# A two-layer hybrid decoder: the weight sums of the block products made in HBM by accumulating DMAs instead of on VectorE

## The chip, the cores and the metric

The kernel runs on one core of a Trainium2 chip. The metric is device time in microseconds (us) from launch to end on that core. Times of unprofiled runs stand beside one profiled execution, from which all views of the trace come.

## What is computed

The reference is a decoder trunk of two layers on 512 tokens of width 1024, in fp32. Cut to what matters here:

```python
def hybrid_layer(x, g_mix, w_in, sinks, w_a, w_b, w_out, g_mlp, w_up, w_down):
    h = rmsnorm(x, g_mix)
    z = h @ w_in                       # 1024 x 5888; q, k, v, retention q, k, v, g, gates a and b
    ...
    ya = sliding_window_sink_attention(aq, ak, av, sinks) @ w_a
    r = chunkwise_retention(rq, rk, rv)
    r = r * lax.rsqrt(jnp.mean(r * r, axis=-1, keepdims=True) + EPS)
    r = r.reshape(B, S, RET_V) * jax.nn.silu(rg)
    yb = r @ w_b                       # 1024 x 1024
    mixed = jax.nn.sigmoid(ga) * ya + jax.nn.sigmoid(gb) * yb
    x = x + mixed @ w_out              # 1024 x 1024
    h2 = rmsnorm(x, g_mlp)
    return x + jnp.square(jax.nn.relu(h2 @ w_up)) @ w_down   # 1024 x 4096 and back
```

The two layers run one after the other, and a last RMS norm follows.

## The kernel before

**Products in three parts.** TensorE (PE) multiplies values rounded to fp32r. To keep fp32's precision each operand is split into a high part `hi` (a rounded copy, made by ACT) and a low part `lo` (the rest, made by VectorE, DVE), and a product is three matmuls: hi by hi, hi by lo, lo by hi (`products`, L332 to L334).

**Weight units.** All weights come as units of 128 x 1024 fp32 (512 KB), 336 in all, in the order that `unit_order` lists: 46 of w_in with 4 of w_a among them, then w_b, w_out, w_up and w_down, for each layer. `load_until` issues a unit's load on SP's queue into one of three buffers `raw`; `split_until` has ACT write `hi` (L286) and DVE `lo` (L287), of which there are three each; `unit` hands them to the matmuls and keeps the split two units ahead and the load three more. SP's queue works in order: a load that waits for its buffer holds back what stands behind it.

**Pairs.** Two units of w_b, w_out or w_up that stand for two blocks of 128 output columns are multiplied as a 2 x 2 block product in Winograd's form, with 7 half products instead of 8: 19 pairs a layer, each in four `part`s. It needs four sums of the weight blocks. With w1 and w2 the two units and L and R their halves of 512 columns, they are s1 = w2R + w2L, s2 = s1 - w1L, s3 = w1L - w2R, s4 = w1R - s2. The same is done with the input (`sum_input`). `narrow_pair` (three matmuls per half product) and `wide_pair` (two: the moving operand holds hi and lo side by side, L1336 and L1337) run the seven products and join the results on DVE.

**Where the sums came from.** For most pairs (`load_part`, `add_part`) the blocks are loaded, and DVE makes the four sums (L252, L255, L259, L260) in the raw buffers and two `big` ones just ahead of the split. Five pairs a layer (`PARKED`) are done ahead: `raws_ahead` loads both units into two `big` buffers, `sums_ahead` has DVE make the sums (L241 to L244), stores them to HBM (L246), and the parts are later loaded from there (L219). `ahead` places this beside retention's projections.

**What sets the order.** The text of the program gives dependences. A scheduler of the framework orders the instructions of each engine by its own estimates, within what the dependences and `issue_after` allow. Attention and retention are generators, advanced between the matmuls of the projections (`advance`), so that PE always has products of weights to fill their waits.

**The other lines that matter.** `silu` (L978, L979) makes the retention gate from ACT's Sigmoid and a DVE multiply. `inverse_rms_halved` makes the factor of the MLP's norm; `first_hooks` calls it after the second unit of the first w_up group. Temporary tiles of 128 x 1024 come from the tag `big`, seven buffers. POOL has nothing to do but a few memsets (L691 clears a tile at the start of each layer) and one product at the end.

Of the kernel before, what the change touches and what calls it, by code (L numbers as in the profile page):

```python
# [18 lines left out]
P = 128  # L19
# [34 lines left out]
PARKED = (("w_b", 0), ("w_b", 2), ("w_out", 6), ("w_up", 4), ("w_up", 6))  # L54
# [73 lines left out]
def decoder(ctx, tc, xT, x_first, w_in, w_a, w_b, w_out, w_up, w_down, tables, decay, band, triangles, g_last, out):  # L128
# [17 lines left out]
    def big(name, dtype=F32):  # L146
        return tmp.tile([P, 2, T], dtype, tag="big", name=name, bufs=7)
# [28 lines left out]
    def raw_tile():  # L176
        return wpool.tile([P, UNIT], F32, tag="raw", name="raw")
# [8 lines left out]
    def load_until(n):  # L186
        while state["loaded"] < min(n, len(order)):
            i = state["loaded"]
            layer, name, j = order[i][:3]
            if name == "pair":  # L190
                load_part(i)
            else:
                raws[i] = raw_tile()
                for at in halves(i):
                    queue = nc.scalar if i == 0 and at.start == 0 else nc.sync
                    queue.dma_start(raws[i][:, at], weights[name][layer, j][:, at])
                    if i < 3:
                        load_x()
            state["loaded"] += 1

# [4 lines left out]

    park = {at: dram.tile([P, 4, T], F32, name="park_%s_%d" % at) for at in PARKED}

    def is_parked(i):
        return order[i][1] == "pair" and (order[i][4], order[i][2]) in park

    def load_part(i):
        layer, _, j, part, src = order[i]
        one, two = (weights[src][layer, j + a] for a in range(2))
        if is_parked(i):
            sums = park[src, j]
            raws[i] = raw_tile()
            sides = ((one[:, LEFT], sums[:, 0, :]), (sums[:, 1, :], one[:, RIGHT]), (sums[:, 2, :], sums[:, 3, :]), (two[:, LEFT],))
            for side, part_of in zip((LEFT, RIGHT), sides[part]):
                nc.sync.dma_start(raws[i][:, side], part_of)  # L219
            return  # L220
        if part == 0:
            raws[i] = raw_tile()
            nc.sync.dma_start(raws[i][:, LEFT], one[:, LEFT])
            raws[i + 3] = raw_tile()
            nc.sync.dma_start(raws[i + 3], two)
        elif part == 1:
            raws[i] = big("raw2").rearrange("p a t -> p (a t)")
            nc.sync.dma_start(raws[i][:, RIGHT], one[:, RIGHT])

    def raws_ahead(layer, src, j):  # L230

        two = [big("ahead").rearrange("p a t -> p (a t)") for _ in range(2)]
        for b, w in enumerate(two):
            nc.sync.dma_start(w, weights[src][layer, j + b])
        return two

    def sums_ahead(src, j, two):

        w1, w2 = two
        s1 = temp("ahead1")  # L240
        nc.vector.tensor_tensor(s1, w2[:, RIGHT], w2[:, LEFT], ALU.add)  # L241
        nc.vector.tensor_tensor(w2[:, RIGHT], w1[:, LEFT], w2[:, RIGHT], ALU.subtract)
        nc.vector.tensor_tensor(w1[:, LEFT], s1, w1[:, LEFT], ALU.subtract)
        nc.vector.tensor_tensor(w1[:, RIGHT], w1[:, RIGHT], w1[:, LEFT], ALU.subtract)  # L244
        for n, part in enumerate((s1, w1[:, LEFT], w2[:, RIGHT], w1[:, RIGHT])):
            nc.sync.dma_start(park[src, j][:, n, :], part)  # L246

    def add_part(i):
        part = order[i][3]
        if part == 0:  # L250
            w2 = raws[i + 3]
            nc.vector.tensor_tensor(raws[i][:, RIGHT], w2[:, RIGHT], w2[:, LEFT], ALU.add)  # L252
        elif part == 1:
            w1 = raws[i - 1]
            nc.vector.tensor_tensor(raws[i][:, LEFT], w1[:, RIGHT], w1[:, LEFT], ALU.subtract)  # L255
        elif part == 2:
            raws[i] = big("raw3").rearrange("p a t -> p (a t)")
            w1, w2, z2 = raws[i - 2], raws[i + 1], raws[i - 1]
            nc.vector.tensor_tensor(raws[i][:, LEFT], w1[:, LEFT], w2[:, RIGHT], ALU.subtract)  # L259
            nc.vector.tensor_tensor(raws[i][:, RIGHT], z2[:, RIGHT], z2[:, LEFT], ALU.subtract)  # L260

    def split_until(n):
        while state["split"] < min(n, len(order)):
            i = state["split"]
            load_until(i + 3)
            paired = order[i][1] == "pair"
            if paired and not is_parked(i):
                add_part(i)
# [19 lines left out]
            raws.pop(i - 3 if paired and not is_parked(i) else i, None)  # L288
# [98 lines left out]
    def group(name, layer, moving, evacuates, meanwhile=None):  # L387
# [3 lines left out]
        for u in range(4):  # L391
            hi, lo = unit(name, layer)
            for j in range(2):
                k = 2 * u + j
                for c, ps in enumerate(banks):
                    cols = slice(j * T + c * P, j * T + (c + 1) * P)
                    products(ps, [((hi[:, cols], lo[:, cols]), moving[k])], k == 0, k == KD - 1)
# [59 lines left out]
    def inverse_rms_halved(both, n, dest):  # L457

        ps = bank(ps_aux, "ssq")
        for i, part in enumerate(both):  # L460
            nc.tensor.matmul(ps, ones, part, start=i == 0, stop=i == len(both) - 1)
# [5 lines left out]
        for rows, cols in sides:  # L467
            for there, _ in sides:
                nc.scalar.activation(dest[there, cols], own[rows, :], AF.Copy)

# [19 lines left out]
    class Rms:  # L490
# [8 lines left out]
        def finish(self):  # L499
            self.value = tmp.tile([P, T], F32, tag="rstd", name="rstd", bufs=2)  # L500
            (inverse_rms if self.folded else inverse_rms_halved)(self.parts, D, self.value)
# [79 lines left out]
    def layer_body(layer):  # L581
# [12 lines left out]
        def sum_input(by_form, b, ks):  # L594
# [1044 lines left out]
```

## Time and profile before

| what | us |
|---|---|
| three runs, median (lowest to highest) | 1472.45 (1472.3 to 1472.51) |
| the profiled execution, its own time | 1473.8 |
| its span, first to last instruction | 1472.0 |
| PE busy | 1464.8 |
| DVE busy | 1166.7 |
| ACT busy | 810.9 |
| DMA, mean share of 16 engines on SP's queue | 40.7% |

The span is what the trace shows; the own time of that execution has 1.8 us more around it. A busy time is the union of an engine's instructions. Matmuls are pipelined and their ends modelled, so two that follow each other overlap in the records. A row such as "L287 DVE TENSOR_TENSOR lo<-raw,hi ... x291 | busy, mean ns | idle before <-releaser" gives a group of instructions: line, engine, operation, what it writes and reads, its count, its busy time, the mean of one in ns, and how long the engine had been idle before them and what ended that.

### The profile page before, as it was taken

The numbers are of one execution on the slowest core, as the hardware profiler recorded it, in microseconds if no ns is written. First come the engines' busy times: TensorE is split into PE (matmuls) and PEld (weight loads), VectorE is DVE, ScalarE is ACT, GpSimd is POOL, SyncE is SP. The second block draws the span as 40 slices with busy tenths as digits, with TensorE's granted clock in tenths as the row PEclk, the third lists the DMA queues.
The fourth block names the chain that finished last, engine by engine and source line by source line (L and its number), as shares of the span: only waits on it lengthen the run. The fifth ranks groups of instructions, "written<-read, shape, count | busy, mean of one in ns | idle before, by whom it ended". The sixth has DMA issues, their size and how long they took to land.

```text
span 1472.0 us, 20220 instructions
## 1 busy us (share of the span) xinstructions
PE 1464.8 (100%) x7466; PEld 1249.6 (85%) x7466; DVE 1166.7 (79%) x1920; ACT 810.9 (55%) x1306; POOL 3.8 (0%) x14
## 2 busy tenths in 40 slices
PE   9999999999999999999999999999999999999998
PEld 7888888888988888888888888888989888888887
DVE  7998878778988787776678986786899877878763
ACT  7656356654684445444455753656547754444553
POOL 0000000000000000000000000000000000000000
PEclk9999999999999999999999999999999999999999
DMA  6422843356443332333543258333654522333241
GB/s 227 127 89 92 300 158 99 102 172 212 126 126 118 101 115 93 104 104 115 165 126 97 86 186 272 104 104 102 207 171 126 154 95 93 114 106 109 90 140 57
DMA packets 71043, 194.45 MB, mean 132 GB/s; under 512 B 8457, under 2 KB 8609, under 8 KB 70945
## 3 DMA queue, kind: packets, MB, share of 16 engines
q1 hardware_dynamic: 70656, 192.65, 40.7%
q8 instruction: 58, 0.95, 0.3%
q10 hardware_dynamic: 288, 0.52, 0.1%
q14 instruction: 41, 0.33, 0.1%
HBM read 171.63 MB, written 18.89 MB: 129 GB/s over the span
## 4 chain that ended last, share of the span: by engine, by line
PE 94%; issue 5%; DMA 1%; DVE 0%; ACT 0%; POOLq 0%; DVEq 0%; SPq 0%
PE mm L334 22%; PE mm L332 22%; PE mm L333 22%; PE mm L1336 11%; PE mm L1337 5%; PE rv L332 2%; PE rv L333 2%; PE rv L334 2%; PE score L842 1%; PE r L332 1%; PE r L334 1%; PE r L333 1%; PE pT L797 0%; PE pv L823 0%; PE pv L824 0%
## 5 line engine op out<-in xcount | busy, mean ns | idle before, releaser
L333 PE MATMUL mm<-r,hi 128*128 128x512 f32 (+1 forms) x1568 | 572.5, 367 | 0.0
L332 PE MATMUL mm<-r,hi 128*128 128x512 f32 (+1 forms) x1568 | 569.7, 367 | 0.6 <-ACT r L342 0.6
L334 PE MATMUL mm<-r,lo 128*128 128x512 f32 (+1 forms) x1568 | 563.9, 367 | 0.2
L286 ACT ACTIVATE hi<-raw 128x1024 fp32r<-128x1024 f32 (+1 forms) x334 | 334.1, 1002 | 386.4 <-PE mm L333 206.8
L287 DVE TENSOR_TENSOR lo<-raw,hi 128x512 fp32r<-128x512 f32 (+1 forms) x335 | 384.7, 1151 | 111.6 <-ACT hi L286 107.9
L334 PEld LDWEIGHTS mm<-r,lo 128*128 128x128 f32 x1568 | 293.7, 188 | 48.7 <-DVE lo L287 1.4
L332 PEld LDWEIGHTS mm<-r,hi 128*128 128x128 f32 x1568 | 293.8, 188 | 47.5 <-ACT r L342 1.4
L333 PEld LDWEIGHTS mm<-r,hi 128*128 128x128 f32 x1568 | 294.3, 188 | 45.9
L1336 PE MATMUL mm<-r,hi 128*128 128x512 f32 x728 | 252.1, 391 | 0.0
L1337 PE MATMUL mm<-r,lo 128*128 128x256 f32 x728 | 200.5, 277 | 0.0
L1336 PEld LDWEIGHTS mm<-r,hi 128*128 128x128 f32 x728 | 136.5, 188 | 28.6
L1337 PEld LDWEIGHTS mm<-r,lo 128*128 128x128 f32 x728 | 136.7, 188 | 3.1 <-DVE lo L287 0.7
L1416 DVE TENSOR_TENSOR x<-x,mm 128x512 f32<-128x512 f32 x56 | 37.8, 686 | 28.9 <-PE mm L334 28.9
L1409 ACT ACTIVATE z<-z 128x512 f32<-128x512 f32 x56 | 32.4, 623 | 48.7 <-DVE z L1389 48.7
L333 PE MATMUL rv<-lo,r 128*128 128x512 f32 x128 | 49.8, 389 | 0.0
L334 PE MATMUL rv<-hi,r 128*128 128x512 f32 x128 | 49.5, 389 | 0.0
L332 PE MATMUL rv<-hi,r 128*128 128x512 f32 x128 | 49.4, 390 | 0.0
L340 DVE TENSOR_TENSOR r<-z,r 128x512 fp32r<-128x512 f32 x64 | 42.9, 686 | 3.0 <-ACT r L339 2.6
L339 ACT ACTIVATE r<-z 128x512 fp32r<-128x512 f32 x64 | 38.4, 619 | 7.9 <-DVE z L1070 7.8
L869 ACT ACTIVATE sm<-sm,st 128x256 f32<-128x256 f32 (+1 forms) x64 | 30.1, 472 | 18.9 <-DVE st L857 18.7
L1389 DVE SCALAR_TENSOR_TENSOR z<-z,rstd 128x512 f32<-128x512 f32 x52 | 35.7, 687 | 0.6
L340 DVE TENSOR_TENSOR r<-sums,r 128x1024 fp32r<-128x1024 f32 x24 | 28.9, 1220 | 0.0
(273 smaller groups left out, 1693.0 us busy)
## 6 DMA issues: line engine op xcount, KB each, us to landing
raw<-w_in_in SPq DMA_DIRECT2D x89, 512.0 KB, 3.7
raw<-w_down_in SPq DMA_DIRECT2D x64, 512.0 KB, 3.6
raw<-w_up_in SPq DMA_DIRECT2D x32, 512.0 KB, 4.0
raw<-w_up_in SPq DMA_DIRECT2D x60, 256.0 KB, 2.9
raw<-w_a_in SPq DMA_DIRECT2D x8, 512.0 KB, 4.8
ahead<-w_b_in SPq DMA_DIRECT2D x8, 512.0 KB, 5.4
park_w_b<-ahead SPq DMA_DIRECT2D x16, 256.0 KB, 5.7
ahead<-w_up_in SPq DMA_DIRECT2D x8, 512.0 KB, 4.9
```

Of the source, the lines that this page charges most:

```text
L286: nc.scalar.activation(hi[:, at], raw[:, at], AF.Copy)
L287: last_low[:] = [nc.vector.tensor_tensor(lo[:, at], raw[:, at], f32(hi[:, at]), ALU.subtract).ins]
L332: nc.tensor.matmul(ps, ah, bh, start=start and i == 0, stop=False, **more)
L333: nc.tensor.matmul(ps, ah, bl, start=False, stop=False, **more)
L334: nc.tensor.matmul(ps, al, bh, start=False, stop=stop and i == n - 1, **more)
L339: nc.scalar.activation(hi, src, AF.Copy)
L340: nc.vector.tensor_tensor(lo, src, f32(hi), ALU.subtract)
L1336: nc.tensor.matmul(both, hi[:, c], m, start=start and k == 0, stop=False, **more)
L1337: nc.tensor.matmul(ps[:, :H], lo[:, c], m[:, 0, :], start=False, stop=k == 3 and start, **more)
L1389: nc.vector.scalar_tensor_tensor(z[:, :, at], z[:, :, at], 0.0, factor, ALU.max, ALU.mult)
L1409: nc.scalar.activation(z[:, i, :], z[:, i, :], AF.Square)
L1416: nc.vector.tensor_tensor(x[:, c, :], x[:, c, :], ps, ALU.add)
```

## The change

All 19 pairs of both layers get their sums from HBM, and no engine adds them. `sum_weights` issues, per pair, four DMAs from HBM to HBM on SP's queue, which copy w2R three times and w1R once into a fresh tensor of four parts, and then five accumulating DMAs on POOL's queue (`accum_op=ALU.add`), each adding 256 KB to a part. [...] The input's second row of sums, the joins, the relu (`ALU.min` for a negated value) and the updates of x take a sign.

When the sums are issued follows from estimated start times of the units (2.45 us for a part of a pair, 5.45 for any other): the n-th pair's at 45 + 33 n us, or 60 us before the estimated load of the pair, whichever is earlier. They stand behind the last load issued by then.

Beside that: four raw buffers instead of three, with loads four ahead of the split; six `big` buffers instead of seven; Silu as one ACT instruction; the end of the MLP's norm (`rms_mlp.finish`) moves into the fourth unit of the first w_up group, with its second half of matmuls held behind the norm's sum.

```diff
-PARKED = (("w_b", 0), ("w_b", 2), ("w_out", 6), ("w_up", 4), ("w_up", 6))
+SUMS_FROM, SUMS_EVERY, SUMS_BEFORE = 45.0, 33.0, 60.0
...
-        return tmp.tile([P, 2, T], dtype, tag="big", name=name, bufs=7)
+        return tmp.tile([P, 2, T], dtype, tag="big", name=name, bufs=6)
...
-        return wpool.tile([P, UNIT], F32, tag="raw", name="raw")
+        return wpool.tile([P, UNIT], F32, tag="raw", name="raw", bufs=4)
...
             state["loaded"] += 1
+            if sums_due and sums_due[0][0] <= starts[i]:
+                with tc.issue_after(last_load[0]):
+                    sum_weights(sums_due.pop(0)[1])
...
+    starts = [0.0]
+    for u in order:
+        starts.append(starts[-1] + (2.45 if u[1] == "pair" else 5.45))
+    pairs_at = [i for i, u in enumerate(order) if u[1] == "pair" and u[3] == 0]
+    sums_due = [(min(starts[i] - SUMS_BEFORE, SUMS_FROM + n * SUMS_EVERY), i) for n, i in enumerate(pairs_at)]
+    sums, last_load = {}, []
+
+    def sum_weights(i):
+
+        layer, _, j, _, src = order[i]
+        one, two = (weights[src][layer, j + a] for a in range(2))
+        dest = dram.tile([P, 4, T], F32, name=f"sums_{src}_{layer}_{j}")
+        s = [dest[:, n, :] for n in range(4)]
+        every = [P, 2, T]
+        for part in s[:3]:
+            nc.sync.dma_start(part, two[:, RIGHT])
+        nc.sync.dma_start(s[3], one[:, RIGHT])
+        for first, block in ((0, two), (1, one)):
+            for n in range(first, first + 2):
+                nc.gpsimd.dma_start(s[n], block[:, LEFT], accum_op=ALU.add)
+        nc.gpsimd.dma_start(s[3], s[1], accum_op=ALU.add)
+        sums[i] = dest
...
+        made = sums.pop(i - 3) if part == 3 else sums[i - part]
+        raws[i] = raw_tile()
+        sides = ((one[:, LEFT], made[:, 0, :]), (made[:, 1, :], one[:, RIGHT]), (made[:, 2, :], made[:, 3, :]), (two[:, LEFT],))
+        for side, part_of in zip((LEFT, RIGHT), sides[part]):
+            last_load[:] = [nc.sync.dma_start(raws[i][:, side], part_of).ins]
...
-            load_until(i + 3)
+            load_until(i + 4)
             paired = order[i][1] == "pair"
-            if paired and not is_parked(i):
-                add_part(i)
...
+                with tc.issue_after(between()) if between and (u, j) == (3, 1) else nullcontext():
+                    for c, ps in enumerate(banks):
...
-            split(*parts_of_forms(0), f[0].rearrange("p (j k) t -> p j k t", k=2))
+            split(*parts_of_forms(0), f[0].rearrange("p (j k) t -> p j k t", k=2), -1.0)
...
-            nc.vector.tensor_tensor(t4, b21, t2, ALU.subtract)
+            nc.vector.tensor_tensor(t4, t2, b21, ALU.subtract)
...
-            ins = nc.vector.tensor_tensor(z[:, 1, SECOND], b, eu[:, :H], ALU.add).ins
+            ins = nc.vector.scalar_tensor_tensor(z[:, 1, SECOND], b, -1.0, eu[:, :H], ALU.mult, ALU.subtract).ins
...
-            s = temp("sig")
-            nc.scalar.activation(s, rg[i], AF.Sigmoid)
-            nc.vector.tensor_tensor(rg[i], rg[i], s, ALU.mult)
+            nc.scalar.activation(rg[i], rg[i], AF.Silu)
...
-                rms_mlp.finish()
-                sum_input(by_form, scaled_pair(2, g_mlp), 2)
...
-                late = group("w_up", layer, xs, [put_up] * 4, first_hooks())
+                late = group("w_up", layer, xs, [put_up] * 4, first_hooks(), rms_mlp.finish)
```

The code of `raws_ahead`, `sums_ahead`, `add_part`, `is_parked` and `ahead` is gone.

More of the change, by code (lines that the diff above doesn't have):

```diff
@@ L1 @@
 from contextlib import ExitStack
+from contextlib import nullcontext
 from functools import partial
@@ L195, in load_until @@
                     queue = nc.scalar if i == 0 and at.start == 0 else nc.sync
-                    queue.dma_start(raws[i][:, at], weights[name][layer, j][:, at])
+                    load = queue.dma_start(raws[i][:, at], weights[name][layer, j][:, at]).ins
+                    if queue is nc.sync:
+                        last_load[:] = [load]
                     if i < 3:
@@ L213, in load_part @@
         one, two = (weights[src][layer, j + a] for a in range(2))
[L214 to L246, printed above, removed]
@@ L385, in chunk, with group @@
         evacuate(ps)
[L387 removed]
+    def group(name, layer, moving, evacuates, meanwhile=None, between=None):
         banks = [bank(ps_mm, "mm") for _ in range(4)]
@@ L460, in inverse_rms_halved @@
         for i, part in enumerate(both):
-            nc.tensor.matmul(ps, ones, part, start=i == 0, stop=i == len(both) - 1)
+            summed = nc.tensor.matmul(ps, ones, part, start=i == 0, stop=i == len(both) - 1).ins
         own = temp("own")[:, : T // 2]
@@ L1126, in layer_body @@
                 silu(i)
-        def ahead():
-            if to_sum:
-                with tc.issue_after(last_low[0]):
-                    sums_ahead(*to_sum.pop(0))
-            load_ahead()
-        qk(1, between=ahead)
-        values(0, ahead)
+        qk(1)
+        values(0)
         aT = [(a_h[:, c, :], a_l[:, c, :]) for c in range(4)]
@@ L1273, in add_to_x, with put @@
         def add_to_x(c):
-            def put(i, at, src, z):
+            def put(i, at, src, z, sign=1.0):
                 own = x[:, c + i, at] if isinstance(i, int) else x[:, c : c + 2, at]
-                return nc.vector.tensor_tensor(own, own, src, ALU.add)
+                return nc.vector.tensor_tensor(own, own, src, ALU.add if sign > 0 else ALU.subtract)
             return put
```

74 lines of the change are left out of this document (28 added, 46 removed).

## The prediction

> **What bounds the kernel now.** I read the page's busy shares and its chain of work first, then the stretches view for the places where TensorE (PE) is not busy, then PE's own waits, then the chain around a gap.
>
> ```profile
> span 1472.0 us, 20220 instructions
> PE 1464.8 (100%) x7466; PEld 1249.6 (85%) x7466; DVE 1166.7 (79%) x1920; ACT 810.9 (55%) x1306; POOL 3.8 (0%) x14
> PE 94%; issue 5%; DMA 1%; DVE 0%; ACT 0%; POOLq 0%; DVEq 0%; SPq 0%
> ```
>
> PE is busy for 1464.8 of 1472.0 us, and the chain that ended last is 94% PE and 5% issue between matmuls. DVE, ACT and DMA hold at most 1% of it. The stretches say where the missing 7.2 us lie; the columns are the stretch, its length, then busy us of PE, PEld, DVE, ACT, POOL, the granted clock, DMA share and GB/s.
>
> ```profile
> 0.00:50.00 50.00, 48.33 (x203) 39.33 (x204) 40.02 (x56) 35.03 (x56) 1.92 (x12) 1.00 0.62 202
> 50.00:350.00 300.00, 300.00 (x1483) 254.46 (x1482) 245.69 (x465) 169.96 (x296) 0.00 (x0) 1.00 0.45 148
> 350.00:400.00 50.00, 49.91 (x331) 45.69 (x330) 46.84 (x69) 29.08 (x43) 0.00 (x0) 1.00 0.48 153
> 400.00:1100.00 700.00, 700.00 (x3473) 593.66 (x3472) 555.40 (x911) 377.92 (x599) 0.96 (x1) 1.00 0.41 132
> 1100.00:1150.00 50.00, 49.91 (x336) 45.88 (x335) 46.41 (x66) 37.73 (x55) 0.00 (x0) 1.00 0.39 117
> 1150.00:1400.00 250.00, 250.00 (x1303) 213.98 (x1302) 196.62 (x299) 128.93 (x196) 0.00 (x0) 1.00 0.35 109
> 1400.00:1472.00 72.00, 66.67 (x348) 56.60 (x346) 35.73 (x61) 32.28 (x61) 0.90 (x1) 0.99 0.29 95
> ```
>
> From 50 to 1400 us PE lacks 0.09 + 0.09 = 0.18 us. The start lacks 1.67 us and the end 5.33 us. A busy PE can hide a short stall, because a matmul's modelled end reaches past the next one's start, so I looked for such stalls in the chain (start us, us, what):
>
> ```profile
> 389.34 0.13 PE mm L334
> ...
> 389.84 0.74 DVE r L343
> ...
> 391.10 1.23 DVE lo L287
> 392.33 0.04 issue
> 392.38 0.38 PE mm L334
> 392.76 0.12 PE mm L332
> ```
>
> One matmul there stands for 0.38 us where its neighbours take 0.12 to 0.13: 0.26 us lost behind DVE, where the MLP of layer 0 begins. I count four such places at most (two at each of the two MLP starts), 1.0 us. So the most that an edit away from start and end can bring is about 0.18 + 1.0 = 1.2 us. The matmuls themselves are the same 7466 in the changed program.
>
> **The change part by part.** *Arithmetic taken off DVE.* Four adds make a pair's sums; 28 pairs make them in place and 10 ahead of time (first and last of each four shown), and 16 gates lose a multiply.
>
> ```profile
> L252 DVE TENSOR_TENSOR raw<-raw 128x512 f32<-128x512 f32 x28 | 19.3, 691 | 7.4 <-DMA raw<-w_up_in 6.5
> L260 DVE TENSOR_TENSOR raw<-raw 128x512 f32<-128x512 f32 x28 | 19.3, 689 | 0.6
> L241 DVE TENSOR_TENSOR ahead<-ahead 128x512 f32<-128x512 f32 x10 | 6.9, 687 | 1.8 <-DMA ahead<-w_up_in 1.6 <-DMA ahead<-w_b_in 0.2
> L244 DVE TENSOR_TENSOR ahead<-ahead 128x512 f32<-128x512 f32 x10 | 6.9, 688 | 0.1
> L979 DVE TENSOR_TENSOR z<-z,sig 128x512 f32<-128x512 f32 x16 | 10.7, 686 | 3.5 <-ACT sig L978 3.5
> L1389 DVE SCALAR_TENSOR_TENSOR z<-z,rstd 128x512 f32<-128x512 f32 x52 | 35.7, 687 | 0.6
> L978 ACT ACT_TABLE_LOAD x2 | 2.6, 1283 | 0.2 <-DVE z L970 0.2
> ```
>
> 4 x 19.3 + 4 x 6.9 + 10.7 = 115 us less of DVE's 1167. Of that PE gets only what it waits for, at most the 1.2 us above; I credit half, 0.6 us, because the stall shown hangs on two DVE steps in a row and only the load beside them gets lighter. The sign edits turn an add into a form with a factor, 687 ns in L1389 for what a plain add of that size takes (686): nothing. *Gates.* Sigmoid becomes Silu, one ACT instruction each as before; by the built program's order ACT loads its function table 23 times instead of 19, 4 x 1.283 = 5.1 us on an engine with 661 us idle. Without that cover it would be 5.1 us.
>
> By the Trainium skill, "ScalarE: Activation LUTs", What ACT_TABLE_LOAD costs, a switch is the 1283 ns load and a drain of about 1380 ns, so 10.7 us by the page. The row agrees on 1283 and shows 0.2 us idle before, so the trace decides for 5.1.
>
> *Buffers.* The fourth weight buffer takes what the seventh "big" buffer gives. Two of the seven served the sums and the loads ahead, which are gone, so six are no tighter: nothing. Should a filler be held up, PE's order has room: the attention's last product comes 31 matmuls after the start of the next stage, before 16; 15 products of at most 0.38 us, 6 us, if nothing ran beside them.
>
> *Moved step.* The end of the MLP's norm goes from the second weight unit to inside the fourth: its sums, square root and copies land beside PE in either place. Nothing; the bound is that 1.0 us of hidden stalls, either way.
>
> *DMA.* This is the large part. Per pair the new code issues four copies HBM to HBM, five accumulating DMAs, and loads seven halves of 256 KB instead of what was 1 MB.
>
> ```profile
> q1 hardware_dynamic: 70656, 192.65, 40.7%
> raw<-w_up_in SPq DMA_DIRECT2D x32, 512.0 KB, 4.0
> raw<-w_up_in SPq DMA_DIRECT2D x60, 256.0 KB, 2.9
> park_w_up<-ahead SPq DMA_DIRECT2D x16, 256.0 KB, 7.3
> ```
>
> 192.65 MB cost 40.7% of 1472 us on all engines, 3.11 us per MB; 256 KB is 0.262 MB. A pair not parked before costs 0.79 MB more to load, 2.4 us; its copies 1.05 MB, 3.3 us; five accumulations of 0.262 MB, 4.1 us if priced as plain transfers. No trace shows an accumulating DMA. It reads two operands and writes one, so its work lies between one plain transfer and three in a row: 4.1 to 12.2 us a pair; a gain is excluded. I take two (8.2), halfway. Its landing lies between a load (2.9) and two loads and a store (2.9 + 2.9 + 7.3 = 13.1); I take 7.3, the row that also writes HBM beside other traffic.
>
> By the Trainium skill, "Collectives: The Full Stack", The bandwidth ceiling, an adding DMA is not slowed by its add but by needing two reads on one ring, which halves its rate. By that page alone a pair's accumulations cost 8.2 us. No run here shows it yet.
>
> What lies beside it, per stretch; the last two lines are pieces of the chain that recur once a pair and two down units:
>
> ```profile
> 300.00:350.00 50.00, 50.00 (x303) 44.70 (x302) 39.40 (x50) 26.19 (x36) 0.00 (x0) 1.00 0.61 197
> 450.00:650.00 200.00, 200.00 (x1018) 170.30 (x1017) 155.39 (x238) 98.83 (x147) 0.00 (x0) 1.00 0.31 101
> 1050.00:1100.00 50.00, 50.00 (x296) 44.43 (x296) 41.89 (x57) 22.70 (x30) 0.00 (x0) 1.00 0.66 218
> ```
>
> ```profile
> 485.57 0.46 PE mm L334 x2
> ...
> 506.06 0.46 PE mm L334 x2
> ```
>
> In the MLP a cycle lasts 506.06 - 485.57 = 20.5 us, 31% of it DMA: 6.4 us, plus 2.4 for the loads. By the rule in the code sums come every 33 us, and for the last six pairs of layer 0 every 20.7. There the sums add 3.3 + 8.2 = 11.5: 20.3 of 20.5 us, full (16.2 at one transfer, 24.3 at three). Elsewhere 11.5 x 20.5/33 = 7.1: 15.9 of 20.5. In the stretches with w_b and w_out, 30.5 to 33 us of 50 are busy; two pairs' loads add 4.8 and 1.5 sums 17: 53 to 55 of 50, late by 3 to 5 us (nothing at one transfer, 9 to 11 at three).
>
> What PE has in hand: four raw buffers and three split ones put a load seven units ahead of PE, six after its buffer comes free. In the MLP six units are 20.5 us, less 4.0 landing and two splits by ACT and DVE:
>
> ```profile
> L287 DVE TENSOR_TENSOR lo<-raw,hi 128x1024 fp32r<-128x1024 f32 x291 | 355.1, 1221 | 105.8 <-ACT hi L286 102.1 <-PE mm L334 1.9 <-DMA ahead<-w_up_in 0.2
> L286 ACT ACTIVATE hi<-raw 128x1024 fp32r<-128x1024 f32 x291 | 307.4, 1058 | 373.2 <-PE mm L333 204.6 <-PE mm L1336 100.5 <-issue 34.0
> SPq L196 <- DVE lo L287: 438.4, 119, 9.5
> ACT hi L286 <- DMA raw<-w_b_in: 6.6, 2, 3.3
> ```
>
> 2 x (1.22 + 1.06) = 4.6: about 12 us in hand. For w_out's parts (24 matmuls of 0.12 us, the fourth part half) six units are 15 us, so about 6. The SP row agrees: SP waits for DVE to free buffers (438 us), while ACT's largest wait for a weight load is 6.6 us in all. So 3 to 5 us late is covered.
>
> *The added waits.* SP waits, before a half made of sums, for POOL's accumulations, with all later weight loads behind it. The code issues sums 60 us or more ahead; copies 7.3 and three accumulations in a row 21.9 make 29: 31 spare. POOL's queue stands twice per pair for a landing and issues five DMAs:
>
> ```profile
> POOL r L691 <- PE mm L1337: 680.4, 1, 680.4
> L691 POOL MEMSET r<- x2: 947/955/963, 0.9 to 683.0; 128x1024 f32 x2
> ```
>
> With at most 0.96 us an issue (POOL's longest row), 14.6 + 4.8 = 19.4 of 20.5 us: it keeps up. The one memset in its way ran at 683 us, when layer 1's first sums begin; they are used some 290 us later. *Sum:* 1472.45 median (the profiled execution: span 1472.0, own time 1473.8, so 0.45 below and 1.35 above) less 0.6 = **1471.8**.
>
> **The rivals.** *A, DMA full (slower):* accumulations cost three transfers. w_b and w_out run 9 to 11 us late against 6 in hand: 3 to 5 lost in each layer, 6 to 10 in all, 1478 to 1482, middle **1480**; with 5 in hand it ends at 1484. In the MLP 24.3 - 20.5 = 3.8 us x 6 = 23 stay inside the 31 spare. It decides from about 2.2 transfers on. For it: the stretches are 61 to 66% busy already. Against: 3.11 us/MB contains queueing.
> *B, POOL's chain (slower):* a landing takes 13.1 us. POOL then needs 26.2 + 1.7 to 4.8 = 28 to 31 us a pair (an issue priced as SP's 0.33 or as 0.96) against 20.5; over six pairs 44 to 63 late, less 60 - 7.3 - 39.3 = 13 spare and 12 in hand: 19 to 38 lost, **1491** to 1510. It decides from about 11 us a landing. Layer 1, at 33 us, escapes. SP's issue row:
>
> ```profile
> 541.96 0.33 SPq L223 DMA_DIRECT2D raw<-w_up_in  x1
> ```
>
> *C, faster by over 0.2%:* would need 2.9 us. Only start and end hold that much, and no edit touches the first load of x or the last stores: **1469** or less.
> *D, the change doesn't spread the sums:* the built order shows 38 groups of copies between weight loads; no chance given.
>
> **How the numbers follow.** Forecast within 0.2% (2.9 us, about what a measurement of this kernel can tell from no change): 0.58. A 0.20, B 0.18, C 0.04. The range runs from full relief of the stalls and a little (1470.3) to A's end (1484) and leaves out B and most of C. Faster 0.04, same 0.58, slower 0.38.
>
> **What would show it.** Right: PE 50.00 of 50.00 from 50 to 1400 us; DVE near 1055 us; DMA share near 1.0 in 550 to 650 and near 0.8 in layer 1's MLP, with weight loads landing within 8 us; no SP wait on sums. A: PE idle in 300 to 400 and 1050 to 1150 with ACT waiting for raw. B: SP waiting on sums and PE idle in 550 to 700 only. Wrong altogether: PE idle near 0 to 300, where I expect none, or another count of matmuls.

## The result and the profile after

The changed kernel takes **1493.11 us** (median of 4 runs, 1492.68 to 1496.41) against 1472.48 (4 runs, 1472.3 to 1473.16): a ratio of **1.0142, 95% interval 1.013 to 1.0154**, 20.6 us slower. The forecast, 1471.8 with a range to 1484, was wrong. The profiled execution took 1493.07 us, with a span of 1491.0.

First the page of the changed kernel: span, busy times, queues (packets, MB, share of 16 engines), and the shares of the chain that ended last.

```profile
span 1491.0 us, 20777 instructions
...
PE 1471.3 (99%) x7466; PEld 1251.9 (84%) x7466; DVE 1061.0 (71%) x1752; ACT 817.7 (55%) x1310; POOL 160.1 (11%) x204
...
q1 hardware_dynamic: 100032, 233.56, 49.5%
q0 software_dynamic: 27360, 49.82, 23.2%
...
PE 87%; DMA 6%; DVE 3%; ACT 2%; issue 1%; SPq 0%; POOLq 0%; ACTq 0%; DVEq 0%
```

The same 7466 matmuls keep PE busy 6.5 us longer in the records and the span grew by 19.0. Of the 6.5 us some 4.5 go with a lower granted clock: its mean over the span fell from 0.999 to 0.996, and 1491 x 0.003 = 4.5, an estimate. The chain was 94% PE and 1% DMA; now it is 87% and 6%, and DVE and ACT hold 5%. The stretches of the changed kernel (columns as before: length, busy PE, PEld, DVE, ACT, POOL, clock, DMA share, GB/s) say where:

```profile
110.00:150.00 40.00, 37.39 (x174) 30.27 (x173) 30.00 (x70) 26.26 (x42) 1.63 (x2) 1.00 0.44 114
...
235.00:245.00 10.00, 9.34 (x42) 7.45 (x41) 6.75 (x10) 4.50 (x9) 0.81 (x1) 1.00 0.49 106
...
370.00:410.00 40.00, 37.20 (x271) 35.42 (x270) 31.60 (x45) 24.21 (x38) 3.29 (x4) 0.96 0.76 208
410.00:780.00 370.00, 369.95 (x1855) 313.99 (x1854) 255.12 (x370) 195.92 (x293) 48.64 (x59) 1.00 0.82 215
...
980.00:1000.00 20.00, 17.51 (x75) 14.33 (x74) 16.63 (x28) 12.16 (x20) 0.81 (x1) 0.91 0.46 118
...
1070.00:1150.00 80.00, 76.14 (x495) 68.64 (x495) 62.30 (x88) 42.49 (x62) 8.20 (x10) 1.00 0.92 255
1150.00:1400.00 250.00, 249.96 (x1294) 213.63 (x1293) 174.04 (x258) 134.31 (x201) 30.43 (x37) 1.00 0.84 211
```

In both MLPs (410 to 780, 1150 to 1400) the DMA engines are 82 and 84% busy and PE lacks 0.05 and 0.04 us. It lacks 2.61 us in attention (110 to 150), 0.66 and 2.49 in retention (235 to 245, 980 to 1000), and 2.80 and 3.86 where w_b and w_out are multiplied (370 to 410, 1070 to 1150), and at 110 to 150 and 980 to 1000 the DMA share is only 0.44 and 0.46. So "DMA full" is not the answer. PE's own waits in the changed kernel (engine, line, waited for: us in total, times, longest):

```profile
PE mm L312 <- ACT mm L622: 3.4, 2, 2.0
PE ret L312 <- DVE s L999: 2.5, 1, 2.5
PE pv L805 <- ACT r L319: 1.9, 2, 1.4
PE mm L312 <- ACT eu L625: 1.8, 2, 1.1
```

PE waits for ACT and DVE, which did not become slower (the product of z with `inv` takes 685 ns, median, before and after). What they waited for stands in the chain, here the pieces ahead of the gap at 990 us (start, us, what):

```profile
963.11 3.32 DMA row<-own
...
966.44 8.70 DMA inv<-row
...
975.17 0.76 DVE z L1046 x2
...
984.00 5.38 DMA inv<-row
...
990.69 0.48 DVE s L999
```

Retention's norm factor goes through HBM and comes back on SP's queue (`inv<-row`, 256 KB), and DVE stands still until it lands. The view of `inv` before gives 3.8 us for its landing; here one takes 8.70. (Such a view holds only landings that it can tie to their issue: for the six of the changed kernel it gives 5.4 at most, and the 8.70 of the chain is not among them. A median of landings is to be read with that in mind.) POOL's instructions at that time (start, us, line, operation, count):

```profile
965.12 2.50 POOL L231 DMA_DIRECT2D sums_w_up<-w_up_in  x3 [21.75 <-DMA sums_w_up<-w_up_in]
976.36 0.81 POOL L231 DMA_DIRECT2D sums_w_up<-w_up_in  x1 [8.74 <-DMA sums_w_up<-w_up_in]
983.57 0.81 POOL L232 DMA_DIRECT2D sums_w_up<-sums_w_up  x1 [6.39 <-DMA sums_w_up<-w_up_in]
```

Three accumulations issued within 2.5 us at 965 stand beside the load issued at 966.44, and the fifth, issued at 983.57, beside the one at 984.00. The gaps at 110 to 150 look alike: the chain ahead of them goes back to the load of a table (`rawtab`), and three accumulations were issued just ahead of it. The piece of the chain, then POOL's instructions:

```profile
105.00 10.56 DMA rawtab<-tables_in
```
```profile
103.47 2.50 POOL L231 DMA_DIRECT2D sums_w_out<-w_out_in  x3 [20.07 <-DMA sums_w_out<-w_out_in]
```

The idle time that ended with a landing of `inv<-row`, in all (us, times), is first in the kernel before, then in the changed one:

```profile
  DMA inv<-row: 8.0, 6
```
```profile
  DMA inv<-row: 19.7, 6
```

By the Trainium skill, "DMA: Bandwidth & Descriptors", Queues, rings and completion order, each DMA engine takes turns packet by packet between the queues that have work. That would make a load on SP's queue late for as long as POOL's queue has packets; the landings of 8.70 and 10.56 us agree, though no trace here shows the order of packets.

### The profile page after: what moved, and what is told of

It is laid out like the page before. It is cut to its first block, busy times and chain, and to the rows that moved or that the text cites. A ratio compares the mean times of both kernels' runs of the same rounds, so it can differ in the third digit from the quotient of the medians.

```text
span 1491.0 us, 20777 instructions
## 1 busy us (share of the span) xinstructions
PE 1471.3 (99%) x7466; PEld 1251.9 (84%) x7466; DVE 1061.0 (71%) x1752; ACT 817.7 (55%) x1310; POOL 160.1 (11%) x204
## 3 DMA queue, kind: packets, MB, share of 16 engines
q0 software_dynamic: 27360, 49.82, 23.2%
## 4 chain that ended last, share of the span: by engine, by line
PE 87%; DMA 6%; DVE 3%; ACT 2%; issue 1%; SPq 0%; POOLq 0%; ACTq 0%; DVEq 0%
PE mm L312 21%; PE mm L313 21%; PE mm L314 21%; PE mm L1299 11%; PE mm L1300 6%; DMA inv<-row 1%; DMA raw<-w_out_in 1%; PE rv L313 1%; PE rv L314 1%; PE rv L312 1%; DVE lo L267 1%; ACT hi L266 1%; DMA rawtab<-tables_in 1%; DMA gate<-aside 1%; DMA row<-own 1%
## 5 line engine op out<-in xcount | busy, mean ns | idle before, releaser
L231 POOL DMA_DIRECT2D sums_w_up<-w_up_in x112 | 92.3, 892 | 659.1 <-DMA sums_w_up<-w_up_in 651.4
L232 POOL DMA_DIRECT2D sums_w_up<-sums_w_up x28 | 22.8, 814 | 167.9 <-DMA sums_w_up<-w_up_in 167.9
```

The source lines that it names most:

```text
L231: nc.gpsimd.dma_start(s[n], block[:, LEFT], accum_op=ALU.add)
```

## The experiments

The theories after the result: **T1**, the sums' DMAs, the accumulations above all, make loads late that DVE, ACT or PE wait for at once. **T2**, the copies stand in SP's queue ahead of those loads. **T3**, one of the other edits. Times are medians; each ratio is against runs of the kernel before on the same chip, at 1472.9 to 1473.0.

| run | us | ratio, 95% interval |
|---|---|---|
| no sums | 1472.62 | 0.9998, 0.9989 to 1.0007 |
| copies only | 1473.98 | 1.0008, 0.9999 to 1.0018 |
| sums in the MLPs only | 1472.34 | 0.9996, 0.9987 to 1.0005 |
| sums outside the MLPs only | 1492.63 | 1.0131, 1.0114 to 1.0148 |
| among w_in only | 1481.68 | 1.0057, 1.0043 to 1.0071 |
| among w_b, w_out only | 1478.85 | 1.0041, 1.0027 to 1.0055 |
| small edits alone | 1475.50 | 1.0018, 1.0009 to 1.0027 |
| plain copies for accumulations | 1476.31 | 1.0024, 1.0015 to 1.0033 |
| four accumulations | 1479.08 | 1.0044, 1.0029 to 1.0059 |
| other places | 1495.22 | 1.0147, 1.0125 to 1.0169 |
| other places, four | 1490.27 | 1.0106, 1.0084 to 1.0128 |
| five, two at once | 1493.89 | 1.0144, 1.0126 to 1.0161 |
| four, three at once | 1488.90 | 1.0122, 1.0099 to 1.0146 |
| four, one at a time | 1494.97 | 1.0147, 1.0123 to 1.0172 |
| four, one at a time, evenly | 1476.61 | 1.0028, 1.0019 to 1.0037 |
| five, evenly | 1488.59 | 1.0099, 1.0084 to 1.0114 |

**No sums; copies only.**

```diff
-        made = sums.pop(i - 3) if part == 3 else sums[i - part]
-        sides = ((one[:, LEFT], made[:, 0, :]), (made[:, 1, :], one[:, RIGHT]), ...)
+        sides = ((one[:, LEFT], two[:, RIGHT]), (two[:, RIGHT], one[:, RIGHT]), ...)
```
```diff
         nc.sync.dma_start(s[3], one[:, RIGHT])
-        for first, block in ((0, two), (1, one)):
-            for n in range(first, first + 2):
-                nc.gpsimd.dma_start(s[n], block[:, LEFT], accum_op=ALU.add)
-        nc.gpsimd.dma_start(s[3], s[1], accum_op=ALU.add)
```

> The changed kernel without the nine DMAs that make a pair's sums: each part of a pair is loaded straight from the weights, so the sums in the products are left out; loads, sign rules, Silu, buffers and the moved norm stay. T1 (the sum DMAs crowd the 16 engines, so that loads which DVE, ACT or PE wait for in the attention, the retention and around w_out land late): 1471 to 1474 us, PE full from 50 to 1400. T2 (the copies stand in SP's queue ahead of those loads): the same, 1471 to 1474. T3 (the loss comes from the other edits: six big buffers, the gates' table loads, the moved norm): 1488 to 1493.

> The changed kernel with the four copies a pair on SP's queue but without the five accumulating DMAs, so the sums are left out. T1: copies are 8 of the 32 points of DMA share that the sums take, so about a quarter of the loss, 1474 to 1481 us. T2: the copies stay in SP's queue, so nearly all of the loss stays, 1487 to 1493. T3: 1488 to 1493.

Without sums the time is that of before, so T3 falls: the buffers, the table loads and the moved norm cost nothing that can be told in this kernel. It is also all that taking 104 us off DVE gives: its page has DVE at 1062.5 and PE still at 1463.9.

```profile
span 1470.5 us, 20199 instructions
...
PE 1463.9 (100%) x7466; PEld 1249.5 (85%) x7466; DVE 1062.5 (72%) x1752; ACT 817.9 (56%) x1310; POOL 3.7 (0%) x14
```

The copies alone cost about 1 us, and the interval holds none as well. That is at the lower edge of T1's 1474 to 1481, so the copies carry less of the loss than their share of the engines. T2 falls; the loss needs the accumulations.

**Where.** The sums are made only where a condition on the load then reached holds; the other pairs' parts come straight from the weights. The edit of the first of four; the others have `not` of this condition, w_in or w_a, and w_b or w_out.

```diff
+                at = sums_due.pop(0)[1]
+                if name == "w_down" or name == "w_up" or (name == "pair" and order[i][4] == "w_up"):
                     with tc.issue_after(last_load[0]):
-                        sum_weights(sums_due.pop(0)[1])
+                        sum_weights(at)
```

> The changed kernel with only those sums (17 of 38) that are issued while MLP weights are being loaded; the other 21 pairs load their parts straight from the weights, so their sums are left out. T1: in the MLP PE waits for nothing but weight loads that run seven units ahead, so 1471 to 1476 us. T2: the same cause would show in the MLP too wherever copies stand ahead of loads, 1472 to 1480. T3: 1488 to 1493.

> The complement: only the 21 sums issued while weights of w_in, w_a, w_b and w_out are being loaded; the other 17 are left out. T1: nearly the whole loss, 1487 to 1493 us, with PE idle in the attention, the retention and around w_out. T2: most of the loss, 1485 to 1493. T3: 1488 to 1493.

> Sums are made only where they fall among the loads of w_in and w_a (attention and retention); the other pairs' parts are loaded straight from the weights, so their sums are left out. Theory that each stretch loses by itself what its late loads cost: the changed kernel lost about 10 us there, so 1481 to 1485. Rival, that the loss comes only when w_b and w_out are loaded: 1472 to 1476.

> Sums are made only where they fall among the loads of w_b and w_out; the other pairs' parts are loaded straight from the weights, so their sums are left out. Theory that each stretch loses by itself: the changed kernel lost about 9 us there, so 1479 to 1484, and the excess of this run and of the one with sums among w_in add up to that of the changed kernel, 20 us. Rival, that attention and retention hold the loss: 1472 to 1476. Rival, that a backlog carried over from w_in makes the loss here: also 1472 to 1476, with the two excesses adding up to less than 15 us.

The 17 sums in the MLPs cost nothing; the other 21 cost all of it (19.6 us). Split by stage they cost 8.7 and 5.9, together 14.6: each stage loses by itself, but w_b and w_out lose a little less than expected (1479 to 1484), and 5 us of the 20 appear only with both. The place of the transfers shifts between these programs, and I did not settle which overlap makes the 5 us.

**The small edits by themselves**, in the kernel before.

```diff
-            nc.scalar.activation(s, rg[i], AF.Sigmoid)
-            nc.vector.tensor_tensor(rg[i], rg[i], s, ALU.mult)
+            nc.scalar.activation(rg[i], rg[i], AF.Silu)
...
-                late = group("w_up", layer, xs, [put_up] * 4, first_hooks())
+                late = group("w_up", layer, xs, [put_up] * 4, first_hooks(), rms_mlp.finish)
```

> The kernel before with two of the small edits alone: Silu as one ACT instruction in place of Sigmoid and a multiply, and the end of the MLP's norm moved into the fourth unit. All is computed. Theory that PE is the bound and that every hidden stall together is worth 1.2 us at most: 1471.3 to 1473.2. Rival, that the four more table loads on ACT or the matmuls held behind the norm's sum cost PE something that the run without sums made up elsewhere: 1474 to 1479.

2.6 us slower, at 1475.5: the rival's side. PE's largest wait in this run:

```profile
PE mm L333 <- ACT mm L643: 2.6, 2, 1.3
```

ACT's instructions in this run, then in the kernel before, at the end of the norm of layer 0:

```profile
425.69 1.68 ACT L471 ACTIVATE rstd<-own 64x256 f32<-64x256 f32 x4
427.39 0.37 ACT L643 ACTIVATE mm<-mm 128x256 f32<-128x256 f32 x1
```
```profile
426.21 0.37 ACT L640 ACTIVATE mm<-mm 128x256 f32<-128x256 f32 x1
426.92 1.70 ACT L469 ACTIVATE rstd<-own 64x256 f32<-64x256 f32 x4 [0.34 <-DVE own L466]
```

The scheduler now puts the norm's four copies ahead of a pair's PSUM copy that PE waits for: 1.3 us, in each layer. In the run without sums the order is the old one, and the loss is not there.

**Adding, or moving bytes?**

```diff
-                nc.gpsimd.dma_start(s[n], block[:, LEFT], accum_op=ALU.add)
+                nc.gpsimd.dma_start(s[n], block[:, LEFT])
...
-        nc.gpsimd.dma_start(s[3], s[1], accum_op=ALU.add)
+        nc.gpsimd.dma_start(s[3], s[1])
```

> The changed kernel with POOL's five DMAs as plain copies of the same 256 KB in the same order, with the same waits; the sums are left out (the parts hold copies of weights). Theory that it is the price of an accumulation (6.94 against 3.16 us of the engines per MB) that fills the engines: half of the added load stays, so 1475 to 1484. Rival, that the bytes, the second queue or POOL's waits matter and adding does not: 1488 to 1495.

1476.31, where the changed kernel has 1493: as many DMAs in the same order, with the same waits and bytes, but without the add, cost 3.4 us and not 20. POOL's queue in this run:

```profile
q0 software_dynamic: 15200, 49.82, 11.5%
```

11.5% of 1474.1 us for 49.82 MB is 3.40 us of the engines per MB; with the add it was 23.2% of 1491.0, 6.94. An accumulation costs 2.04 plain copies on the same queue. POOL's part is shorter too, 103.6 us busy against 160.1. That it takes nothing from DVE the busy times show: DVE has 1061.0 us in the changed kernel, 1061.1 here and 1062.5 without sums, where POOL has 3.7.

**Fewer accumulations; other places.** The first edit copies the second sum (w2R + w2L + w1L) from the finished first one (w2R + w2L) and then adds the last term. The second moves sums out of w_b and w_out and into layer 0's MLP.

```diff
-        for part in s[:3]:
+        for part in (s[0], s[2]):
             nc.sync.dma_start(part, two[:, RIGHT])
...
+        nc.gpsimd.dma_start(s[0], two[:, LEFT], accum_op=ALU.add)
+        nc.gpsimd.dma_start(s[2], one[:, LEFT], accum_op=ALU.add)
+        nc.gpsimd.dma_start(s[1], s[0])
+        nc.gpsimd.dma_start(s[1], one[:, LEFT], accum_op=ALU.add)
         nc.gpsimd.dma_start(s[3], s[1], accum_op=ALU.add)
```
```diff
+    early = [45.0 + 25.0 * n for n in range(8)]
+    late = [595.0 + 20.7 * n for n in range(5)] + [740.0, 800.0, 860.0]
+    due = early + [starts[i] - SUMS_BEFORE for i in pairs_at[8:19]] + late + [starts[i] - SUMS_BEFORE for i in pairs_at[27:]]
```

> The changed kernel with four accumulations and one plain copy on POOL's queue in place of five accumulations, and three copies on SP's in place of four: the second sum is copied from the finished first one, and the first weight row added to it. All is computed. Theory that the loss goes with the engines' time in accumulations: a fifth of the 20 us goes, 1486 to 1491. Rival, that what matters is that some sum is always under way beside the late loads: the same time as the changed kernel, 1491 to 1496.

> The changed kernel with the same 38 sums at other places: in layer 0 eight among the loads of w_in (seven before) and none among those of w_b and w_out; five of layer 1's moved into layer 0's MLP, three left among layer 1's w_in loads (eight before) and none among its w_b and w_out. All is computed. Theory that it is the place which decides: 11 sums among w_in at the 8.7 us that 15 cost there, or a little less where they stand further apart, and nothing else: 1477 to 1481. Rival, that the amount of DMA in the whole program decides: 1490 to 1495. Rival, that the MLP of layer 0, now with sums every 20.7 us throughout, becomes full and loses: 1484 or more with PE idle in 400 to 780.

> Both at once: the other places and four accumulations. All is computed. Theory of place and of the time in accumulations: 1476 to 1480, a little under the run with the places alone. It does not come under the kernel before (1473), as the run with sums in the MLP alone already equalled it.

All three miss the figures of the theory. With four the time is 1479: 14 of 20 us gone for a fifth of the accumulations, while POOL's queue still holds the engines for 22.7% of 1476.7, 335 us against 346. A loss in proportion to the engines' time falls. (Outside the MLPs PE lacks 0.9 us in layer 0 and 2.6 in layer 1.) The other places cost as much as the changed kernel; the stretches of that run tell why:

```profile
50.00:400.00 350.00, 349.91 (x1815) 300.26 (x1813) 272.88 (x499) 202.89 (x342) 28.64 (x35) 1.00 0.65 171
400.00:780.00 380.00, 374.46 (x1869) 316.26 (x1868) 256.85 (x372) 197.35 (x294) 68.86 (x83) 1.00 0.97 240
780.00:1150.00 370.00, 369.28 (x1902) 315.93 (x1901) 284.32 (x511) 215.72 (x357) 13.14 (x16) 1.00 0.51 144
1150.00:1400.00 250.00, 242.30 (x1237) 205.17 (x1236) 163.03 (x245) 124.25 (x187) 43.04 (x52) 0.99 0.97 233
```

Outside the MLPs PE lacks 0.09 and 0.72 us, with fewer sums there (8 and 3), though still three accumulations at once: as a cure for the late loads it worked. But with a sum every 20.7 us throughout, the MLPs' engines are 97% busy and PE lacks 5.5 and 7.7 us there. SP waits for weight loads to land (75.6 us in the largest row of its waits) and hardly for sums (2.4). That is the third expectation of that run, a second way to lose: full engines, the prediction's rival A in another place. With both edits (1490.27; runs from 1483.59 to 1491.11) PE lacks 4.75 us in layer 0's MLP at 91%, and 0.04 in layer 1's at the same 91%, so a share alone does not tell the loss here either.

**How many at once, or the fifth?** In the changed kernel POOL issues three in a row; with four accumulations, two, then one plain copy and two single ones. The three edits below: five with two at once; four with three at once; four one at a time (`add` stands for the accumulate option).

```diff
-        for first, block in ((0, two), (1, one)):
-            for n in range(first, first + 2):
-                nc.gpsimd.dma_start(s[n], block[:, LEFT], accum_op=ALU.add)
-        nc.gpsimd.dma_start(s[3], s[1], accum_op=ALU.add)
+        first = nc.gpsimd.dma_start(s[1], two[:, LEFT], accum_op=ALU.add).ins
+        with tc.issue_after(first):
+            beside = nc.gpsimd.dma_start(s[0], two[:, LEFT], accum_op=ALU.add).ins
+        with tc.issue_after(beside):
+            second = nc.gpsimd.dma_start(s[1], one[:, LEFT], accum_op=ALU.add).ins
+        with tc.issue_after(second):
+            third = nc.gpsimd.dma_start(s[2], one[:, LEFT], accum_op=ALU.add).ins
+        with tc.issue_after(third):
+            nc.gpsimd.dma_start(s[3], s[1], accum_op=ALU.add)
```
```diff
-        nc.gpsimd.dma_start(s[3], s[1], accum_op=ALU.add)
```
```diff
+        last = nc.gpsimd.dma_start(s[0], two[:, LEFT], accum_op=ALU.add).ins
+        for dest_, src_, more in ((s[1], s[0], {}), (s[1], one[:, LEFT], add), (s[3], s[1], add), (s[2], two[:, RIGHT], {}), (s[2], one[:, LEFT], add)):
+            with tc.issue_after(last):
+                last = nc.gpsimd.dma_start(dest_, src_, **more).ins
```

> The changed kernel with its five accumulations per pair, the same bytes and the same copies, but in an order on POOL's queue in which at most two are under way at once for most of the time: the first on the second sum beside the one on the first sum, then the second on the second sum beside the one on the third, then the last. In the changed kernel POOL issues three in a row. All is computed. Theory of how many are under way at once (what a late load finds ahead of it): near the run with four accumulations, 1478 to 1484. Rival, that it is the fifth accumulation itself, its time on the engines: 1490 to 1495.

> The changed kernel without the last accumulation of each pair (the fourth sum lacks its second term), the other four in the order of the changed kernel, three of them issued in a row. Theory of how many are under way at once: most of the loss stays, 1486 to 1493. Rival, that the fifth accumulation itself makes it: near the run with four accumulations, 1476 to 1482.

> Four accumulations and two plain copies on POOL's queue, each waiting for the one before but for the copy of the third sum's first term, which runs beside the fourth sum's accumulation; one copy of the first sum's term and one of the fourth's stay on SP's queue. All is computed. Theory of how many are under way at once: less than with four accumulations in pairs (1479), 1474 to 1478. Rival, that only the time on the engines counts: the same 1478 to 1481, as the bytes and the accumulations are the same.

Four with three at once lose 16 us, as the number at once says and the fifth accumulation does not. But five with two at once lose as much as the changed kernel, so two are no better than three when they follow each other in pairs. And one at a time took 1495, against 1474 to 1478 expected. Its stretches, first of early work, then of layer 0's MLP (two views):

```profile
50.00:250.00 200.00, 200.00 (x946) 167.35 (x945) 153.04 (x329) 115.04 (x215) 22.54 (x31) 1.00 0.64 151
...
800.00:1150.00 350.00, 349.90 (x1811) 300.40 (x1810) 265.72 (x474) 197.59 (x324) 37.82 (x53) 1.00 0.66 172
```
```profile
600.00:720.00 120.00, 107.08 (x512) 90.15 (x511) 64.28 (x98) 47.40 (x72) 14.90 (x20) 0.93 0.68 171
```

In 50 to 250 PE lacks nothing, and 0.10 us in 800 to 1150, which holds all of layer 1's attention, retention and w_out. The changed kernel lacked 3.27 in the first of these stretches with no more DMA:

```profile
50.00:250.00 200.00, 196.73 (x925) 163.50 (x924) 150.80 (x325) 113.64 (x212) 20.45 (x25) 1.00 0.62 153
```

What PE lacks in this run, 12.9 us, it lacks at 600 to 720. The clock there was 0.93, which is 120 x 0.07 = 8.4 us more, an estimate from that row; together they come near the 22 us that the run lost. POOL's first accumulations of three pairs in a row, and SP's wait for sums:

```profile
571.41 1.14 POOL L228 DMA_DIRECT2D sums_w_up<-w_up_in  x1
...
601.27 1.12 POOL L228 DMA_DIRECT2D sums_w_up<-w_up_in  x1
...
630.88 1.12 POOL L228 DMA_DIRECT2D sums_w_up<-w_up_in  x1
```
```profile
SPq L241 <- DMA sums_w_up<-w_up_in: 54.5, 9, 13.7
```

A pair's chain takes 29.6 to 29.9 us, and layer 0's last six pairs come every 20.5: SP waits for POOL, with all weight loads behind it. That is the prediction's rival B. So the sums were spaced evenly, first with one at a time, then in the changed kernel:

```diff
-SUMS_FROM, SUMS_EVERY, SUMS_BEFORE = 45.0, 33.0, 60.0
+SUMS_FROM, SUMS_EVERY, SUMS_BEFORE = 45.0, 29.0, 60.0
```

> The run with one accumulation at a time, with a pair's sums every 29 us of the code's estimate instead of every 33, so that layer 0's last six pairs no longer follow each other at 20.7. All is computed. Theory: that run lost nothing in attention, retention and around w_out (349.90 of 350 us of PE in 50 to 400, where the changed kernel has 353.93 of 360) and 21 us at 600 to 800 because POOL's chain takes 29.6 us a pair against the 20.5 of the MLP's pace; 29 of the estimate are 31 of the trace, so POOL keeps up: 1472 to 1477, PE full from 50 to 1400. Rival, that it lost nothing early only by chance of where the transfers fell: 1480 or more with PE idle in attention or retention again.

> The changed kernel with a pair's sums every 29 us of the code's estimate instead of every 33 and nothing else: five accumulations, three issued in a row. All is computed. Theory that it is what runs at once and not the spacing: no gain, 1488 to 1497. Rival, that the spacing makes the difference: under 1480.

1476.61 and 1488.59, each inside its range. The stretches of the run with one at a time, then those of the run with five and three at once:

```profile
50.00:400.00 350.00, 349.38 (x1807) 299.32 (x1806) 271.15 (x498) 203.45 (x342) 43.50 (x60) 1.00 0.73 182
...
780.00:1150.00 370.00, 369.90 (x1905) 316.88 (x1905) 286.73 (x506) 215.22 (x352) 47.84 (x66) 1.00 0.74 186
```
```profile
50.00:400.00 350.00, 349.72 (x1816) 300.04 (x1815) 272.70 (x499) 203.43 (x342) 41.02 (x50) 1.00 0.74 191
...
780.00:1150.00 370.00, 357.99 (x1836) 304.94 (x1835) 270.99 (x483) 202.06 (x334) 42.13 (x52) 1.00 0.72 183
```

At the same DMA shares, 0.74 and 0.72, the one lacks 0.10 us of PE at 780 to 1150 and the other 12.01. But the other lost only 0.28 in layer 0, 50 to 400. So several accumulations at once are a risk, not a fixed price: what they cost seems to depend on whether they fall on one of the few loads that are waited for, and that shifts with every edit. Taking each layer's work outside its MLP as one case (PE's missing time at 50 to 400 and at 780 to 1150): the changed kernel lost 5.4 and 6.8, five with two at once 2.1 and 10.7, four with three at once 6.1 and 3.7, four with two at once 0.9 and 2.6, five evenly 0.3 and 12.0; one at a time lost 0.1 and 2.3 (that after its backlog), and evenly 0.6 and 0.1. That waiting for each other protects those loads is likely, but not shown: these are three cases without a backlog, three at once lost as little in one case here and in the run with other places, and the chained runs also have four accumulations where the others mostly have five, and fewer copies on SP's queue. No run has five in a chain. Why five in pairs are as bad as threes is open too, and no run tells which overlap is the decisive one.

The best full form of the change, 1476.6, is still 3.6 us above the kernel before; its stretches show 1 us of it as PE's missing time. Against the run without sums its span is 4.0 us longer, and 2.1 of that lie within PE's busy time (1466.0 against 1463.9); what makes them I have not located. None beats the kernel before: the run without any sums shows nothing to be had, by its interval at most 1.6 us.

## Why the prediction was wrong

- *PE bounds the kernel, and DVE's relief is worth 1.2 us at most:* right. Without the sums 1472.62 against 1473.0, no difference that can be told; DVE at 1061 against 1055 expected (the working's own 115 us would have left 1052; 106 went).
- *Gates:* ACT went from 810.9 to 817.7 us, 6.8 against 5.1, and hidden. *Buffers:* nothing, right. *Moved norm:* nothing in this kernel, but 2.6 us in the kernel before, above the bound of 1.0 that was given "either way": a moved step changed ACT's order.
- *Price of an accumulation, two plain transfers:* right, 2.04 on one queue. By the Trainium skill, "Collectives: The Full Stack", The bandwidth ceiling, a ReduceScatter among ranks reaches about half the rate of an AllGather, because its add needs two source reads on one ring. The 2.04 agrees with that factor; it is for transfers within HBM issued by one core.
- *Landing 7.3 us, POOL keeps up, SP hardly waits for sums:* right. The landing of most of POOL's accumulations in the changed kernel (count, KB, median us), and SP's largest wait for sums (us in total, times, longest):

```profile
sums_w_up<-w_up_in POOLq DMA_DIRECT2D x112, 256.0 KB, 7.9
```
```profile
SPq L242 <- DMA sums_w_up<-w_up_in: 3.0, 5, 1.5
```

- *The MLP nearly full without loss:* right, at 0.82 and 0.84, and even at 0.97 in 550 to 600. But its 20.3 of 20.5 us "full" without loss held only for a few pairs: when the sums came every 20.7 us throughout, 97% cost PE 13 us.
- **The step that failed: "What PE has in hand".** It measured the slack of weight loads, which run seven units ahead, and set all added DMA against that. For "Elsewhere" it took 15.9 of 20.5 us busy and stopped there. It left out the loads with little or nothing in hand, which DVE or ACT waits for: `inv<-row`, `rawtab`, the gates. The trace before had `inv<-row` plainly: DVE was idle 8.0 us in all for it, six times, so a later landing went straight to DVE (19.7 us in the changed kernel) and, where the fillers ran out, to PE. The others it did not show as waits, or hardly (`rawtab` 0.2 us, the gates none); what they had in hand was never measured, and it did not cover landings of 10 us (5.5 us and 9.2 us of DVE's waits). Where the prediction had PE full it lacked 5.4 us at 50 to 400 and 6.8 at 780 to 1150. "Wrong altogether: PE idle near 0 to 300, where I expect none" is what came, at 110 to 150 and 235 to 245.
- *w_b and w_out, "late by 3 to 5 us, covered by 6":* wrong. A backlog of the engines' time was computed, but what hit was single landings. A half of w_out, issued at 394, took 10.55 us, 6.5 more than the 4.0 reckoned with, against 6 in hand (the pieces of the chain ahead of PE's wait, below); gates brought back (`gate<-aside`) at 1070 took 10.41, and PE waited 1.0 us behind them:

```profile
394.39 10.55 DMA raw<-w_out_in
...
405.04 0.63 ACT hi L266
405.67 0.28 ACT eu L625
```

- *Rivals.* A had the resource and the direction, and its sign came in part: PE lacks 2.1 us in 300 to 400 and 3.9 in 1050 to 1150, and ACT waits 6.0 us in all for w_out's loads. But its price, its condition (2.2 transfers) and its place (w_b and w_out alone) were wrong. B did not happen in the changed kernel, and did happen where the chain was made longer.

## What to carry to other kernels

Before adding background DMA, list the transfers that are waited for at once, and judge the addition by their landing times. Here an engine share of 0.44 to 0.49 went with late loads, and one of 0.84 cost nothing where every load ran well ahead. Letting large background transfers wait for each other rather than issuing them in a row is worth a try (the best form here did), as long as the chain so formed keeps the pace at which its results are needed. And where the engine relieved of work isn't the bound, look for a gain elsewhere: here the work moved could only cost.

## What the runs showed of the hardware

- An accumulating DMA from HBM to HBM took 2.04 times the engines' time of a plain one on the same queue: 6.94 against 3.40 us per MB.
- After the gap of PE at 988 to 991 us the granted clock was lower for some microseconds (the column before the last two):

```profile
986.00:991.00 5.00, 2.73 (x13) 1.92 (x12) 2.02 (x4) 0.42 (x1) 0.00 (x0) 1.00 0.51 111
991.00:996.00 5.00, 4.79 (x15) 3.97 (x16) 5.00 (x11) 3.10 (x6) 0.00 (x0) 0.66 0.34 105
```

At 0.66 of the clock 5 us of matmuls are 5 x 0.34 = 1.7 us longer, an estimate from these rows: this gap of some 2.3 us is nearly paid for twice. It is no rule: in the run with five, evenly, a gap of 3.4 us (1032.6 to 1036.0) was followed by 5 us at a clock of 1.00.
